# First loads alone, the rest by GpSimd; norm of the input in written order, first two projections by quarters of the tokens

## The chip, the cores and the metric

The kernel runs on one core of one Trainium2 chip. Its time is the device time of one execution in microseconds. Before the change the median of 3 runs is 2382.75 us (2381.59 to 2386.46).

## The reference

A decoder trunk of two layers over 1024 tokens with 1024 channels, float32. In each layer the input is normalized (RMS norm with a gain), projected by one matrix to 3072 columns, and these columns go to four groups of heads: a gated convolution over 31 tokens, a stick-breaking attention, a retention in chunks of 128 tokens and a short gated convolution. The groups' outputs are joined, projected back and normalized, and added to x. A feed-forward part with a convolution over 3 tokens follows.

```python
h = rms_norm(x, norm_mix_pre[l])
proj = h @ w_in[l]                       # 1024 x 1024 by 1024 x 3072
(c_a, c_gate, sb_q, sb_k, sb_v, r_q, r_k, r_v, r_g,
 sc_b, sc_c, sc_h) = jnp.split(proj, N_IN_SLICES, axis=-1)
...
x = x + rms_norm(mix, norm_mix_post[l])
f = conv_ffn(rms_norm(x, norm_ffn_pre[l]), ffn_up[l], ffn_conv_w[l], ffn_down[l])
x = x + rms_norm(f, norm_ffn_post[l])
```

The change concerns `h` and the first 2 of the 24 column blocks of `proj`, in the first layer only.

## The kernel before, in words

**Operands in two parts.** Each float32 operand of a large product is split into a high part, rounded to the type that TensorE multiplies fast, and the remainder. `split` (L180) casts the high part on ScalarE (L181) and subtracts on VectorE (L182). A product is then three: high by high, high by low, low by high. `hH` and `hL` hold the normalized input, transposed, in 8 tiles of 128 tokens.

**The start (L551 to L576).** For each of the 8 tiles of 128 tokens a load of 512 KB from SyncE's queue (L560), `norm` (L165: on ScalarE a sum of squares at L151, logarithm at L156, exponential at L158; on VectorE the scaling by factor and gain at L167), eight transposes on TensorE (L177, against the identity `ident`) into an accumulator or a `tp` tile, as `X0` says, and the split. The identity and the gain (one row of 4 KB, read 128 times by one load, L186) are issued behind the first tile. At the fifth tile the first two weights are fetched (`prefetch`, L201, which calls `load_weight`, L189: a load of 512 KB into the one buffer `wr`, the cast L193, the subtraction L195 into `wh` and `wl`, two buffers each). Params and constants (L571 to L574) are issued last.

**The order of the work.** The program is a list of instructions. A planner gives each engine its own fixed order by estimated starting times, priorities and the order of the text; within `tc.manual_schedule` the named engines keep the order of the text. Each engine works through its own list and waits at an instruction whose operands or whose place aren't ready. `tc.issue_after(ins)` puts all that a block issues on that instruction's engine behind it.

**The projections.** A projection takes one weight of 1024 x 128 (8 blocks of 128 x 128) and gives 128 columns for all 1024 tokens, in one accumulator of two banks. The first two are made as a pair (`project_pair`, L228, called at L716 in both layers): 24 products of 512 tokens for each of two halves of the tokens and each of two weights, 96 in all. The others follow singly (`project`, L216), their accumulators in turn 0 and 1 (`project(n % 2, ...)`, L726); from the third on TensorE keeps the order of the text (L719). `prefetch` fetches one weight ahead. The first projection gives keys (`stick_k`, L333: for each half of the rows a split from the accumulator, L340, and two loads that copy the parts to the other 64 partitions, L341 and L342), the second gives queries (`stick_q`, L324: L328 on ScalarE, L329 on VectorE), the third values. An accumulator is given to its next user when all instructions that read it are done. The scores of the attention (`stick_scores`, L346: products at L361 and L362, the mask at L364) come in between the products of the third and later projections, at slots that are counted in eighths of a projection.

**Buffers.** `ualloc` and `ufree` (L114, L121) hand out 29 buffers of 512 KB in turn.

Of the kernel before, what the change touches and what calls it, by code (L numbers as in the profile page):

```python
# [7 lines left out]
F32 = mybir.dt.float32  # L8
F32R = mybir.dt.float32r
# [3 lines left out]
P = 128  # L13
D = 1024
T = 1024
KT = D // P
NB = T // P
# [53 lines left out]
WPOOL = []  # L71
UPOOL = ()
SKEW = 0
# [3 lines left out]
XP = 4  # L77
OB = 3
FB = 2
X0 = (0,1,2,None,2,None,2,None)  # L80
# [3 lines left out]


@with_exitstack
def trunk_kernel(ctx, tc, x, w_in, w_out, w_up, w_down, params, gains, consts, rope, out):
    nc = tc.nc
    const = ctx.enter_context(tc.tile_pool(name="const", bufs=1))
    big = ctx.enter_context(tc.tile_pool(name="big", bufs=1))  # L90
    wp = ctx.enter_context(tc.tile_pool(name="wp", bufs=2))
    small = ctx.enter_context(tc.tile_pool(name="small", bufs=8))
    pt = ctx.enter_context(tc.tile_pool(name="pt", bufs=2, space=bass.MemoryType.PSUM))
# [3 lines left out]
    ident = const.tile([P, P], F32, name="ident")  # L97
    par = const.tile([P, DEPTH * NPAR], F32, name="par")
    tri = const.tile([P, P], F32, name="tri")
    ones_c = const.tile([P, P], F32, name="ones_c")  # L100
    ones_b = const.tile([P, P], F32, name="ones_b")
    mask = const.tile([P, P], F32, name="mask")
    gam = const.tile([P, 2], F32, name="gam")
# [10 lines left out]
    def ualloc(dt=F32, shape=(P, T)):  # L114
        s = free.pop(0)
        count[0] += 1
        t = big.tile(list(shape), dt, tag=f"u{s}", name=f"u{s}_{count[0]}")
        slot_of[id(t)] = (s, t)
        return t

    def ufree(*ts):  # L121
        for t in ts:
            free.append(slot_of.pop(id(t))[0])
# [11 lines left out]
    def ptile(slot, shape=(P, T)):  # L135
        pcount[0] += 1
        return pp[0].tile(list(shape), F32, tag=f"pp{slot}", name=f"pp{slot}_{pcount[0]}")
# [7 lines left out]
    hH = const.tile([P, NB, KT, P], F32R, name="hH")  # L145
    hL = const.tile([P, NB, KT, P], F32R, name="hL")
    xs = [dr.tile([T, D], F32, name=f"xs{i}") for i in range(2 * DEPTH - 1)]

    def square_sum(src, junk):
        ss = stile("ss")  # L150
        nc.scalar.activation(junk, src, AF.Square, accum_out=ss)  # L151
        return ss

    def rstd_of(ss):
        ln = stile("ln")
        nc.scalar.activation(ln, ss, AF.Ln, scale=1.0 / D, bias=eps_t)  # L156
        r = stile("r")
        nc.scalar.activation(r, ln, AF.Exp, scale=-0.5)  # L158
        return r
# [5 lines left out]
    def norm(xt, gbc, hh):  # L165
        r = rstd_of(square_sum(xt, hh))
        nc.vector.scalar_tensor_tensor(hh, xt, r, gbc, ALU.mult, ALU.mult)  # L167

    def transpose_h(t, hh, slot):
        n = 4 if slot is None else KT  # L170
        for k in range(0, KT, n):
            if slot is None:
                tp = pt.tile([P, 4, P], F32, tag="t", name="tp")
            else:
                tp = ptile(slot, (P, KT, P))
            for j in range(n):
                nc.tensor.transpose(tp[:, j, :], hh[:, (k + j) * P:(k + j + 1) * P], ident)  # L177
            split(hH[:, t, k:k + n, :], hL[:, t, k:k + n, :], tp)

    def split(h, l, src):  # L180
        nc.scalar.copy(h, src)  # L181
        nc.vector.tensor_sub(l, src, h.bitcast(F32))  # L182

    def gain(i):
        g = ualloc()
        nc.sync.dma_start(g, gains[i].partition_broadcast(P))  # L186
        return g

    def load_weight(src, eng):  # L189
        raw = wp.tile([P, KT, P], F32, tag="wr", name="wr", bufs=WR)  # L190
        nc.sync.dma_start(raw, src)
        wh = wp.tile([P, KT, P], F32R, tag="wh", name="wh")
        nc.scalar.copy(wh, raw)  # L193
        wl = wp.tile([P, KT, P], F32R, tag="wl", name="wl")
        eng.tensor_sub(wl, raw, wh.bitcast(F32))  # L195
        return wh, wl

    queue = []
    ready = []

    def prefetch(n=1):  # L201
        while queue and len(ready) < n:
            with tc.high_priority(offset=HPW):
                ready.append(load_weight(*queue.pop(0)))

    def project_kt(ps, w, kt, halves):
        wh, wl = w
        for w, m in ((wh, hH), (wh, hL), (wl, hH)):
            for half in halves:
                nc.tensor.matmul(  # L210
                    ps[:, half * 512:(half + 1) * 512], w[:, kt, :],
                    m[:, 4 * half:4 * half + 4, kt, :],
                    start=(kt == 0 and m is hH and w is wh),
                    stop=(kt == KT - 1 and w is wl))
# [13 lines left out]
    def project_pair(slots):  # L228

        prefetch(2)  # L230
        ws = [ready.pop(0), ready.pop(0)]
        ps = [ptile(i) for i in slots]
        for half in range(2):
            for p, w in zip(ps, ws):
                for kt in range(KT):
                    project_kt(p, w, kt, (half,))
                if half:
                    prefetch()
        return ps
# [182 lines left out]
    def rope_load(i):  # L422
        c = ualloc()
        nc.sync.dma_start(c, rope[i, 0])
        s = ualloc()
        nc.sync.dma_start(s, rope[i, 1])
        return c, s
# [122 lines left out]

    psum("pp")  # L551
    nc.scalar.preload_act_table_set("natural_log_exp_and_others")
    queue += [(w_in[0, n], nc.gpsimd if n in WPOOL else nc.vector) for n in range(24)]
    hhs = []
    for t in range(NB + SKEW):
        if t == XP:
            prefetch(2)
        if t < NB:
            xt = ualloc()
            nc.sync.dma_start(xt, x[t * P:(t + 1) * P, :])  # L560
            if t == 0:
                nc.sync.dma_start(ident, consts[0])
                g_pre = gain(0)
            hhs.append(ualloc())
            norm(xt, g_pre, hhs[t])
            ufree(xt)
        if t >= SKEW:
            transpose_h(t - SKEW, hhs[t - SKEW], X0[t - SKEW])
            ufree(hhs[t - SKEW])
    ufree(g_pre)  # L570
    nc.sync.dma_start(par, params)  # L571
    for dst, i in ((mask, 1), (tri, 2), (ones_c, 3), (ones_b, 4)):
        nc.sync.dma_start(dst, consts[i])
    nc.sync.dma_start(gam, consts[5, :, 0:2])  # L574
    nc.vector.tensor_copy(identr, ident)
    nc.vector.tensor_copy(maskr, mask)  # L576

# [1 line left out]
    for l in range(DEPTH):  # L579
# [133 lines left out]
        at(LN_SLOT + LN_VAR, lambda: layer_var(L, y, sq))  # L713
        cs = None
        region = ExitStack()
        pair = project_pair((0, 1))  # L716
        for n, (kind, i, col) in enumerate(IN_ORDER):
            if n == REGION:
                region.enter_context(tc.manual_schedule(engines={mybir.EngineType.PE}))  # L719
            if kind in ("rq", "rk"):  # L720
                cs = rope_load((0 if kind == "rq" else 2) + i)
# [42 lines left out]
        g_post, g_pre = gain(4 * l + 1), gain(4 * l + 2)  # L764
# [278 lines left out]
        with tc.manual_schedule(engines={mybir.EngineType.PE}):  # L1043
            nextw = weight_pairs(NPLAIN)
            next(nextw)
            w = list(nextw)
            psum("xyz")
            for j in range(NPLAIN, NF):
# [7 lines left out]
                w = ffn_products(j, w, sums, nextw, freed if end else lambda n: None)  # L1056
# [7 lines left out]
        for ci, ch in enumerate(chunks):  # L1064
            final = ci == len(chunks) - 1
            if final:
# [3 lines left out]
                g_post, g_pre = gain(4 * l + 3), None if last else gain(4 * l + 4)  # L1070
# [91 lines left out]
```

## Time and profile before

| | |
|---|---|
| median of 3 runs | 2382.75 us |
| the profiled execution | 2386.67 us, span 2384.9 us |
| TensorE (PE) busy | 2297.3 us, 96% |
| its weight loads (PEld) | 1885.0 us, 79% |
| VectorE (DVE) | 1674.2 us, 70% |
| ScalarE (ACT) | 1080.7 us, 45% |
| GpSimd (POOL) | 196.5 us, 8% |
| DMA | 209.87 MB, mean 88 GB/s |
| mean granted clock of TensorE | 0.986 |

Engines are named as in the profile: PE, PEld (TensorE's weight loads), DVE, ACT, POOL, SP (SyncE). A row of the timeline has its start in us, its length in us, the engine, the line of the kernel, the operation, what it writes and reads, how many instructions are merged in it, and in brackets the idle time of the engine before it and what ended that. [...]

### The profile page before, as it was taken

What the parts mean: (1) busy time and instruction counts of PE and PEld (TensorE: products, weight loads), DVE (VectorE), ACT (ScalarE), POOL (GpSimd) and SP (SyncE); (2) the same over time, 40 slices, a digit from 0 to 9 for tenths busy, and PEclk for the clock granted to TensorE, in tenths of its full rate; (3) what the DMA queues carried; (4) which work ended last, traced back from release to release, by engine and by line L of the source; (5) the groups of instructions that cost most, each with busy time, mean ns of one, the idle gap of its engine ahead of it and who ended that gap; (6) DMA issues with size and microseconds to landing.
All of it is one profiled execution on the core that took longest, in us unless ns stands there. A gap on an engine that the chain in (4) does not pass through costs nothing.

```text
span 2384.9 us, 26334 instructions
## 1 busy us (share of the span) xinstructions
PE 2297.3 (96%) x10596; PEld 1885.0 (79%) x10596; DVE 1674.2 (70%) x1749; ACT 1080.7 (45%) x1463; POOL 196.5 (8%) x84
## 2 busy tenths in 40 slices
PE   7998999999999999999999989999999999999998
PEld 6876787787888888788778767877888888888886
DVE  4699877559777777644556998775598777774445
ACT  5663565434455445421246535654344554453112
POOL 0000000000000000643210000000000000016420
PEclk9998999999999999999999989999999999999999
DMA  4212212412122224522222122123122222235223
GB/s 150 71 53 63 62 36 88 138 48 92 68 88 89 80 80 143 183 80 98 80 80 71 53 62 62 36 95 135 53 89 80 80 80 89 87 121 176 84 71 124
DMA packets 58810, 209.87 MB, mean 88 GB/s; under 512 B 7104, under 2 KB 7872, under 8 KB 58688
## 3 DMA queue, kind: packets, MB, share of 16 engines
q1 hardware_dynamic: 58688, 208.19, 26.7%
q8 instruction: 83, 1.36, 0.2%
q14 instruction: 39, 0.32, 0.0%
HBM read 159.93 MB, written 39.85 MB: 84 GB/s over the span
## 4 chain that ended last, share of the span: by engine, by line
PE 38%; DVE 7%; ACT 3%; DMA 1%; issue 1%; DVEq 0%; SPq 0%
PE pp L984 10%; PE pp L210 9%; PE ppx L901 8%; PE ppy L901 4%; DVE u L261 2%; PE ppz L901 2%; PE pp L738 1%; DVE u L182 1%; ACT u L151 1%; DMA wr<-in_w_out 1%; PE op L409 1%; DVE u L379 1%; DVE u L167 1%; PE tp L396 0%; DMA wr<-in_w_up 0%
## 5 line engine op out<-in xcount | busy, mean ns | idle before, releaser
L261 DVE SCALAR_TENSOR_TENSOR u<-u,par,u 128x1023 f32<-128x1023 f32 (+10 forms) x280 | 356.3, 1284 | 28.6 <-ACT u L793 24.4
L210 PE MATMUL pp<-hH,wh 128*128 128x512 f32 x960 | 327.2, 411 | 1.0 <-DVE u L182 0.5
L997 DVE TENSOR_TENSOR u<-u,pp 128x1024 f32<-128x1024 f32 x143 | 174.6, 1221 | 209.9 <-PE pp L984 209.8
L210 PE MATMUL pp<-hL,wh 128*128 128x512 f32 x960 | 312.7, 396 | 0.0
L210 PE MATMUL pp<-hH,wl 128*128 128x512 f32 x960 | 311.5, 395 | 0.0
L984 PE MATMUL pp<-u,u 128*128 128x512 f32 x1152 | 266.0, 392 | 6.1 <-ACT u L955 4.6
L984 PEld LDWEIGHTS pp<-u,u 128*128 128x128 f32 x1152 | 216.6, 189 | 52.4 <-ACT u L955 5.4
L974 POOL TENSOR_TENSOR hH<-u,hH 128x1024 fp32r<-128x1024 f32 x24 | 58.1, 2451 | 1946.5 <-ACT hH L973 1946.5
L210 PEld LDWEIGHTS pp<-hL,wh 128*128 128x128 f32 x960 | 183.6, 191 | 40.4
L210 PEld LDWEIGHTS pp<-hH,wl 128*128 128x128 f32 x960 | 183.2, 191 | 40.3
L210 PEld LDWEIGHTS pp<-hH,wh 128*128 128x128 f32 x960 | 172.6, 193 | 37.5 <-issue 5.9
L738 PE MATMUL pp<-u,hH 128*128 128x512 f32 x512 | 140.2, 392 | 0.4 <-ACT u L181 0.4
L984 PE MATMUL pp<-hH 128*128 128x512 f32 x576 | 131.5, 389 | 0.0
L984 PEld LDWEIGHTS pp<-hH 128*128 128x128 f32 x576 | 108.1, 188 | 22.4
L901 PE MATMUL ppx<-u,wh 128*128 128x512 f32 x384 | 118.4, 389 | 0.3 <-ACT u L926 0.3
L793 ACT ACTIVATE u<-u,par 128x1024 f32<-128x1024 f32 x76 | 87.8, 1156 | 67.4 <-DVE u L947 65.6
L738 PEld LDWEIGHTS pp<-u,hH 128*128 128x128 f32 x512 | 95.0, 188 | 20.4 <-ACT u L181 1.2
L195 DVE TENSOR_TENSOR wl<-wr,wh 128x1024 fp32r<-128x1024 f32 x60 | 73.3, 1221 | 50.9 <-ACT wh L193 50.7
L973 ACT CAST u<-u 128x1024 fp32r<-128x1024 f32 x48 | 50.2, 1052 | 128.9 <-DMA u<-in_w_down 85.7
L901 PE MATMUL ppx<-u,hH 128*128 128x512 f32 x352 | 108.4, 389 | 0.0
L193 ACT CAST wh<-wr 128x1024 fp32r<-128x1024 f32 x60 | 63.0, 1051 | 71.3 <-PE pp L210 57.1
L379 DVE TENSOR_TENSOR_SCAN u<-pp,u 128x1023 f32<-128x1023 f32 (+3 forms) x64 | 87.8, 1403 | 0.7
(240 smaller groups left out, 4400.3 us busy)
## 6 DMA issues: line engine op xcount, KB each, us to landing
wr<-in_w_up SPq DMA_DIRECT2D x50, 512.0 KB, 3.5
wr<-in_w_in SPq DMA_DIRECT2D x48, 512.0 KB, 3.5
gd<-u SPq DMA_DIRECT2D x44, 512.0 KB, 2.9
u<-in_w_down SPq DMA_DIRECT2D x44, 512.0 KB, 4.3
u<-gd SPq DMA_DIRECT2D x44, 512.0 KB, 3.9
u<-in_w_up SPq DMA_DIRECT2D x38, 512.0 KB, 4.3
xs<-u SPq DMA_DIRECT2D x24, 512.0 KB, 2.6
u<-xs SPq DMA_DIRECT2D x24, 512.0 KB, 3.4
```

The costliest lines, as they stand in the source:

```text
L193: nc.scalar.copy(wh, raw)
L195: eng.tensor_sub(wl, raw, wh.bitcast(F32))
L210: nc.tensor.matmul(ps[:, half * 512:(half + 1) * 512], w[:, kt, :], m[:, 4 * half:4 * half + 4, kt, :], start=(kt == 0 and m is hH and w i ...
L261: eng.scalar_tensor_tensor(acc[:, lo:hi], src[:, lo - s:hi - s], wc, acc[:, lo:hi], ALU.mult, ALU.add)
L379: nc.vector.tensor_tensor_scan(rev, z[:, o + 1:e + 1][:, ::-1], rev, r[:, e:e + 1], ALU.add, ALU.add)
L738: nc.tensor.matmul(ps[:, hs], a[:, t, k, :], w[:, hs], start=(k == 0 and a is hH and w is wo[k][0]), stop=(k == KT - 1 and a is hL))
L793: nc.scalar.activation(acc, ps, AF.Copy, scale=par[:, w + 2:w + 3])
L901: nc.tensor.matmul(ps, a[:, kt, :], x(m, kt), start=start and kt == 0 and a is wh and m == 0, stop=kt == 3 and a is wl, skip_group_check=True)
L973: nc.scalar.copy(h, raw)
L974: (nc.gpsimd if len(loads) >= 4 else nc.vector).tensor_sub(lo, raw, h.bitcast(F32))
L984: nc.tensor.matmul(ps[:, hs], a[:, ts_], w[:, hs], start=(i == 0 and w is h and a is gh), stop=(i == len(gs) - 1 and a is gl))
L997: nc.vector.tensor_add(facc[t], facc[t], ps)
```

## The change

The gain of the first norm comes as an array of its own, `gain0`, with 128 equal rows. SyncE issues four loads: the first tile of x, the gain, the second tile, the identity. GpSimd copies one element of the first tile (`held`), which waits for that tile, and behind it issues the other tiles of x and the first two weights in the order written, then the third weight, params and the constants. The tiles of x and the two weights each have a buffer of the 29. The three engines TensorE, ScalarE and VectorE run the start in the written order of `step`: N is a norm, X the transposes of a tile, S its split, W a weight's split, M(i, q) the 24 products of projection i over quarter q of the tokens (256 of them), each with a moving operand of 256 columns instead of 512. In the first layer this pair takes the place of `project_pair`.

```diff
--- before.py
+++ after.py
@@ -84,7 +84,7 @@
 
 
 @with_exitstack
-def trunk_kernel(ctx, tc, x, w_in, w_out, w_up, w_down, params, gains, consts, rope, out):
+def trunk_kernel(ctx, tc, x, w_in, w_out, w_up, w_down, params, gains, gain0, consts, rope, out):
     nc = tc.nc
     const = ctx.enter_context(tc.tile_pool(name="const", bufs=1))
     big = ctx.enter_context(tc.tile_pool(name="big", bufs=1))
@@ -186,9 +186,9 @@
         nc.sync.dma_start(g, gains[i].partition_broadcast(P))
         return g
 
-    def load_weight(src, eng):
+    def load_weight(src, eng, dma=None):
         raw = wp.tile([P, KT, P], F32, tag="wr", name="wr", bufs=WR)
-        nc.sync.dma_start(raw, src)
+        (dma or nc.sync).dma_start(raw, src)
         wh = wp.tile([P, KT, P], F32R, tag="wh", name="wh")
         nc.scalar.copy(wh, raw)
         wl = wp.tile([P, KT, P], F32R, tag="wl", name="wl")
@@ -550,28 +550,87 @@
 
     psum("pp")
     nc.scalar.preload_act_table_set("natural_log_exp_and_others")
-    queue += [(w_in[0, n], nc.gpsimd if n in WPOOL else nc.vector) for n in range(24)]
-    hhs = []
-    for t in range(NB + SKEW):
-        if t == XP:
-            prefetch(2)
-        if t < NB:
-            xt = ualloc()
-            nc.sync.dma_start(xt, x[t * P:(t + 1) * P, :])
-            if t == 0:
-                nc.sync.dma_start(ident, consts[0])
-                g_pre = gain(0)
-            hhs.append(ualloc())
-            norm(xt, g_pre, hhs[t])
-            ufree(xt)
-        if t >= SKEW:
-            transpose_h(t - SKEW, hhs[t - SKEW], X0[t - SKEW])
-            ufree(hhs[t - SKEW])
+    xts, raws, hhs, tps, ws0 = {}, [], {}, {}, []
+
+    def load_x(t, eng):
+        xts[t] = ualloc()
+        eng.dma_start(xts[t], x[t * P:(t + 1) * P, :])
+
+    def load_w(eng):
+        raws.append(ualloc(F32, (P, KT, P)))
+        eng.dma_start(raws[-1], w_in[0, len(raws) - 1])
+
+    load_x(0, nc.sync)
+    g_pre = ualloc()
+    nc.sync.dma_start(g_pre, gain0)
+    load_x(1, nc.sync)
+    nc.sync.dma_start(ident, consts[0])
+
+    held = nc.gpsimd.tensor_copy(const.tile([1, 1], F32, name="held"), xts[0][0:1, 0:1])
+    with tc.issue_after(held.ins):
+        load_x(2, nc.gpsimd)
+        load_w(nc.gpsimd)
+        load_x(3, nc.gpsimd)
+        load_w(nc.gpsimd)
+        for t in range(4, NB):
+            load_x(t, nc.gpsimd)
+
+    def begin_norm(t):
+        hhs[t] = ualloc()
+        norm(xts[t], g_pre, hhs[t])
+        ufree(xts[t])
+
+    def begin_transpose(t):
+
+        if X0[t] is None:
+            tps[t] = [pt.tile([P, 4, P], F32, tag="t", name="tp") for _ in range(2)]
+        else:
+            tps[t] = [ptile(X0[t], (P, KT, P))]
+        for k in range(KT):
+            n = KT // len(tps[t])
+            nc.tensor.transpose(tps[t][k // n][:, k % n, :], hhs[t][:, k * P:(k + 1) * P], ident)
+
+    def begin_split(t):
+        n = KT // len(tps[t])
+        for i, tp in enumerate(tps[t]):
+            split(hH[:, t, i * n:(i + 1) * n, :], hL[:, t, i * n:(i + 1) * n, :], tp)
+        ufree(hhs[t])
+
+    def begin_weight(i):
+        wh = wp.tile([P, KT, P], F32R, tag="wh", name="wh")
+        wl = wp.tile([P, KT, P], F32R, tag="wl", name="wl")
+        split(wh, wl, raws[i])
+        ufree(raws[i])
+        ws0.append((wh, wl))
+
+    pair0 = []
+
+    def begin_product(i, quarter):
+
+        if quarter == 0:
+            pair0.append(ptile(i))
+        wh, wl = ws0[i]
+        cs = slice(256 * quarter, 256 * quarter + 256)
+        for n, (w, m) in enumerate(((wh, hH), (wl, hH), (wh, hL))):
+            for kt in range(KT):
+                nc.tensor.matmul(pair0[i][:, cs], w[:, kt, :], m[:, 2 * quarter:2 * quarter + 2, kt, :],
+                                 start=(n == 0 and kt == 0), stop=(n == 2 and kt == KT - 1))
+
+    with tc.manual_schedule(engines={mybir.EngineType.PE, mybir.EngineType.Activation, mybir.EngineType.DVE}):
+        N, X, S, W, M = begin_norm, begin_transpose, begin_split, begin_weight, begin_product
+        for step in ((N, 0), (X, 0), (N, 1), (S, 0), (X, 1), (N, 2), (W, 0), (S, 1), (X, 2), (M, 0, 0),
+                     (N, 3), (W, 1), (S, 2), (X, 3), (M, 1, 0), (N, 4), (S, 3), (X, 4), (M, 0, 1),
+                     (N, 5), (S, 4), (X, 5), (M, 1, 1), (N, 6), (S, 5), (X, 6), (M, 0, 2), (N, 7), (S, 6),
+                     (X, 7), (M, 1, 2), (S, 7), (M, 0, 3), (M, 1, 3)):
+            step[0](*step[1:])
     ufree(g_pre)
-    nc.sync.dma_start(par, params)
-    for dst, i in ((mask, 1), (tri, 2), (ones_c, 3), (ones_b, 4)):
-        nc.sync.dma_start(dst, consts[i])
-    nc.sync.dma_start(gam, consts[5, :, 0:2])
+    queue += [(w_in[0, n], nc.vector, nc.gpsimd if n == 2 else nc.sync) for n in range(2, 24)]
+    with tc.issue_after(held.ins):
+        prefetch()
+        nc.gpsimd.dma_start(par, params)
+        for dst, i in ((mask, 1), (tri, 2), (ones_c, 3), (ones_b, 4)):
+            nc.gpsimd.dma_start(dst, consts[i])
+        nc.gpsimd.dma_start(gam, consts[5, :, 0:2])
     nc.vector.tensor_copy(identr, ident)
     nc.vector.tensor_copy(maskr, mask)
 
@@ -713,7 +772,7 @@
         at(LN_SLOT + LN_VAR, lambda: layer_var(L, y, sq))
         cs = None
         region = ExitStack()
-        pair = project_pair((0, 1))
+        pair = project_pair((0, 1)) if l else pair0
         for n, (kind, i, col) in enumerate(IN_ORDER):
             if n == REGION:
                 region.enter_context(tc.manual_schedule(engines={mybir.EngineType.PE}))
@@ -1150,6 +1209,7 @@
     arrays, args = {}, []
     for name, v in (("x", a["x"].reshape(T, D)), ("w_in", w_in), ("w_out", a["w_out"]), ("w_up", w_up),
                     ("w_down", a["ffn_down"]), ("params", np.concatenate(par, axis=1)), ("gains", gains),
+                    ("gain0", np.broadcast_to(gains[0], (P, D))),
                     ("consts", consts), ("rope", rope)):
         v = np.ascontiguousarray(v)
         arrays["in_" + name] = v
```

## Rows read from the trace of the kernel before

**Rows 1.** Stretches: the start, and one of the first layer.

```profile
0.00:22.35 22.35, 7.27 (x32) 6.24 (x32) 10.38 (x11) 15.10 (x32) 0.20 (x4) 1.00 0.72 256
...
110.00:260.00 150.00, 130.16 (x640) 106.05 (x639) 143.52 (x160) 73.46 (x94) 0.00 (x0) 0.93 0.22 64
```

**Rows 2.** Timeline of the start, all engines.

```profile
4.49 1.06 ACT L151 ACTIVATE u<-u 128x1024 f32<-128x1024 f32 x1 [2.47 <-DMA u<-in_x]
...
6.00 0.20 ACT L158 ACTIVATE r<-ln 128x1 f32<-128x1 f32 x1
8.72 1.28 DVE L167 SCALAR_TENSOR_TENSOR u<-u,r,u 128x1024 f32<-128x1024 f32 x1 [3.79 <-DMA u<-in_gains]
...
10.06 1.97 PE L177 MATMUL pp<-ident,u 128*128 128x128 f32 x8 [10.06 <-DVE u L167]
...
12.57 0.99 ACT L181 CAST hH<-pp 128x1024 fp32r<-128x1024 f32 x1
...
13.59 1.23 DVE L182 TENSOR_TENSOR hL<-pp,hH 128x1024 fp32r<-128x1024 f32 x1 [0.65 <-ACT hH L181]
...
22.35 0.50 PE L210 MATMUL pp<-hH,wh 128*128 128x512 f32 x1 [0.50 <-ACT hH L181]
...
25.63 0.90 PEld L177 LDWEIGHTS tp<-ident,u 128*128 128x128 f32 x8 [0.17 <-issue]
...
26.50 0.19 PEld L210 LDWEIGHTS pp<-hH,wl 128*128 128x128 f32 x1
```

**Rows 3.** Stretches of half a microsecond: the DMA engines.

```profile
5.50:6.00 0.50, 0.00 (x0) 0.00 (x0) 0.00 (x0) 0.43 (x4) 0.00 (x0) 1.00 0.91 238
...
8.50:9.00 0.50, 0.00 (x0) 0.00 (x0) 0.28 (x1) 0.00 (x0) 0.00 (x0) 1.00 1.02 418
```

**Rows 4.** Timeline of SyncE's queue.

```profile
3.55 0.44 SPq L191 DMA_DIRECT2D wr<-in_w_in  x1
...
9.90 0.33 SPq L571 DMA_DIRECT2D par<-in_params  x1
```

**Rows 5.** Groups by line: GpSimd's costliest (busy us, mean ns).

```profile
L974 POOL TENSOR_TENSOR u<-u,u 128x1024 fp32r<-128x1024 f32 x32 | 76.5, 2405 | 58.1 <-PE pp L984 27.4 <-ACT u L973 22.4 <-issue 8.1
```

**Rows 6.** Timeline of TensorE: products of 512 and of 256 columns.

```profile
73.03 0.62 PE L210 MATMUL pp<-hH,wl 128*128 128x512 f32 x2
73.48 1.12 PE L409 MATMUL op<-u,u 128*128 128x256 f32 x8
74.43 0.63 PE L210 MATMUL pp<-hH,wh 128*128 128x512 f32 x2
```

**Rows 7.** Timeline: eviction of the first projection, start of the third.

```profile
42.90 1.06 ACT L193 CAST wh<-wr 128x1024 fp32r<-128x1024 f32 x1 [9.12 <-PE pp L210]
...
43.86 1.00 ACT L181 CAST u<-pp 64x1024 fp32r<-64x1024 f32 x1
...
45.13 1.21 DVE L182 TENSOR_TENSOR u<-pp,u 64x1024 fp32r<-64x1024 f32 x1
...
46.38 1.01 ACT L181 CAST u<-pp 64x1024 fp32r<-64x1024 f32 x1 [1.51 <-DVE u L182]
...
47.42 1.23 DVE L182 TENSOR_TENSOR u<-pp,u 64x1024 fp32r<-64x1024 f32 x1 [1.08 <-ACT u L181]
...
48.79 0.70 PE L210 MATMUL pp<-hH,wh 128*128 128x512 f32 x2 [0.27 <-DVE u L182]
```

**Rows 8.** Stretches: two waits of TensorE and what follows each.

```profile
953.73:956.74 3.01, 0.00 (x1) 0.01 (x1) 2.97 (x4) 3.01 (x5) 0.00 (x0) 0.98 0.42 161
956.74:960.30 3.56, 3.56 (x9) 2.84 (x10) 3.56 (x2) 2.79 (x3) 2.59 (x2) 0.54 0.00 0
...
583.28:588.96 5.68, 0.00 (x1) 0.03 (x1) 5.65 (x6) 2.58 (x3) 0.00 (x0) 0.91 0.14 57
588.96:595.00 6.04, 6.04 (x15) 4.74 (x16) 2.41 (x3) 0.54 (x1) 0.00 (x0) 0.52 0.21 87
```

**Rows 9.** Timeline of TensorE: the first scores.

```profile
55.71 0.39 PE L361 MATMUL pp<-u,u 128*128 128x512 f32 x1
```

## The prediction

> **What bounds the kernel now.** I read the page's first part (TensorE is far ahead of the rest), then stretches of the start, then the timeline of that stretch, then TensorE's waits. In the first 22.35 us TensorE is idle for 15.1; from 110 to 260 VectorE is full (143.5 of 150 us) and TensorE waits for it [rows 1]. The change touches only the first 49 us. The timeline shows what ends last there [rows 2]: the first tile of x is there at 4.49, its norm's factor at 6.20, but the scaling waits for the gain until 8.72; the transposes begin at 10.06, and the first product, over tokens 0 to 511, at 22.35. The third projection starts at 48.79. All later work follows TensorE's order from that point: VectorE's long convolutions feed on projections still to come, so a shift at 48.79 moves the full stretch too. What I forecast is the shift of that one start.
>
> **Loads.** The gain is now read from an array with 128 rows instead of one row 128 times. While it was under way the DMA engines were busy 0.91 at 238 GB/s; behind it 1.02 at 418 [rows 3]. At 418 GB/s a 512 KB tile takes 1.3 us, so behind x0 (4.5) I put the gain at 5.8, x1 at 7.1, the identity at 7.2. The other loads wait for x0 on GpSimd and queue there: a one-element copy, then x2, w0, x3, w1, x4 to x7, the third weight, params and constants. SyncE is rid of 15 issues of 0.33 to 0.44 us [rows 4]. GpSimd issues no DMA in this trace. The bounds for one issue there are SyncE's 0.33 us and the 2.4 us of GpSimd's nearest instruction [rows 5]; up to 1.3 the wire hides it. I take 1.3: x2 8.5, w0 9.8, x3 11.1, w1 12.4, then one per 1.3. Worked through at 2.4, the end of the stage moves by 0.1 us only, since TensorE uses one tile in some 3.8 us.
>
> [...]
>
> **The written order.** A norm is 1.71 us on ScalarE (4.49 to 6.20), the scaling 1.28, eight transposes 1.97 at the slow clock and, once warm, 0.87 to their successor; a split is 1.0 on ScalarE and 1.23 on VectorE [rows 2], a weight the same. In order: norm 0 ready 6.2, scaled 7.5, transposed 7.55 to 9.5. Norm 1 from 7.1, scaled 10.1, transposed 10.15 to 12.1. ScalarE: split 0 at 9.6, norm 2 at 10.5 (scaled 13.5), weight 0 at 12.1, split 1 at 13.05. Transposes 2 from 13.55 to 15.5, and there the first quarter begins: 15.5 against 22.35. Its last third needs the low half of split 1, done by 16, so it doesn't stop.
>
> A product of 256 columns costs 0.119 us to its successor (eight from 73.48 to 74.43), one of 512 0.226 (two from 73.03) [rows 6]. Thus 192 halves instead of 96 wholes is 22.9 against 21.7 us, 1.2 more. A quarter is 24 x 0.119 = 2.87 us.
>
> [...]
>
> The first quarter, partly at the slow clock, I give 0.3 more: it ends at 18.7. Behind it stand, back to back, five tiles' transposes (5 x 0.92 = 4.6) and six quarters (17.2): the fourth quarter of projection 0 ends at 40.5, that of projection 1 at 43.3. Norms and splits (2.7 us of ScalarE and 2.5 of VectorE a tile) stay ahead of TensorE's 3.8. Bounds: the clock full already at 12 gives 39.3 for projection 0, not before 19 gives 41.9.
>
> **The new wait.** Projections 0 and 2 share an accumulator (slot n % 2), so the third can't start before all of the first is evicted. Before, the first ended at 42.90, and one piece followed another: third weight cast 42.90, key high 43.86, low 45.13, high 46.38, low 47.42 to 48.65, TensorE on at 48.79 [rows 7]: 5.9 us. The second projection's last half lay over it (24 x 0.226 = 5.4 us), so only 0.4 us were lost. Now only a quarter, 2.87 us, lies over it. TensorE stands from 43.3 until 40.5 + 5.9 = 46.4. If ScalarE takes the first query's piece (1.0 us like the key's, ready at 43.4) ahead of the second key's, both engines lose some 0.75 more: 47.1. If the key went ahead of the weight, it would be 1 earlier: 45.4. I take 46.8, a gain of 2.0 us, not the 5 by which the products end earlier. Behind the waiting product stands everything of TensorE; nothing else is ready for it, since scores need the queries.
>
> **The clock.** TensorE would stand for 3.5 us. [...]
>
> **Moved without cost.** The constants and params come by GpSimd after x7, some 17 to 25 us; the mask's first use is with the scores at 55.71, 6.9 behind the third projection's start [rows 9]. The key's low half is sent to its other partitions at about 44 and needed at 53.7. The third weight's cast needs the buffer of weight 0, free at 40.5, and lies in the eviction chain counted above. One input more changes nothing inside the span.
>
> **Sum.** -2.0 + 1.8 = -0.2 us. The profiled execution, 2386.67 for a span of 2384.9, stands 3.9 above the median 2382.75 of runs between 2381.59 and 2386.46; the difference applies to any of them: 2382.5. What a measurement can tell from no change is 0.2%, 4.8 us.
>
> **Rivals.**
> (1) The stage is quicker and the wait shorter. With the clock up by 14 us projection 0 ends at 39.6; with the key cast first the third starts at 44.5, 4.3 earlier, after 2.1 us of standing, over which the clock may hold: 2378.4. For it: both are choices of a planner and of the clock that the rows don't fix. Against it: before, the weight went first [rows 7].
> (2) Slower: GpSimd's issues become the bound. Above about 2.5 us for each of its first eight loads they set the stage, since weight 1 and the tiles then come later than TensorE asks; from there on the change is slower than before. At 3.5 us (x2 10.7, w0 14.2, x3 17.7, w1 21.2) projection 0 ends at 46.0 and the third starts at 52.1, 3.3 late; with the clock's 1.8, 2387.9. [...]
> (3) It does as said, but the planner, whose starting times have changed, orders VectorE's and ScalarE's work otherwise between 110 and 260, where VectorE is full: one piece of 1.2 us more or less ahead of each of some four waits of TensorE is 5 us either way, 2378 or 2388. Against it: behind the third projection the same work stands in the same order, only shifted.
>
> **How the numbers follow.** Forecast 0.60, (1) 0.17, (2) 0.13, (3) 0.10. The forecast's own bounds: third start 45.2 to 48.2, loss by the clock 0 to 2.9, so 2379 to 2385; 0.04 of its 0.60 lies over 4.8 us faster, 0.03 slower. Faster by over 0.2%: 0.04 + half of (1), 0.09, + 0.06 of (3) = 0.19. Slower: 0.03 + 0.08 of (2) + 0.04 of (3) = 0.15. Within: 0.66. The range takes in the forecast, (1) but for its end, and (2) up to 3.5 us an issue: 2376.5 to 2388.
>
> **What would show it.** The first scaling at about 6.2, the first product near 15.5, the last of the pair near 43. Then one wait of TensorE on VectorE's split, 3 us long, where there was 0.3, with the third projection's first products 0.44 apart. If the third starts by 45 at the full clock, (1) holds; if norms wait for x3 to x7, (2). Wrong altogether would be a third projection that starts as the pair's products end, 43.5, or a difference that arises behind 110 us.

## The result, and the profile after

| | median us | lowest to highest | runs |
|---|---|---|---|
| before | 2384.61 | 2381.59 to 2386.62 | 4 |
| after | 2407.6 | 2401.16 to 2411.72 | 4 |

The ratio is 1.0095, with a 95% interval from 1.0069 to 1.0121: 23 us slower, where no change was forecast. The profiled execution is the fastest of the four (2401.16 us, span 2399.4) and stands against one of before that was among its slowest (2386.67), so the two traces show 14.5 us of the 23.

The start went nearly as forecast. The timeline of the changed kernel (the columns of [rows 2]), its start and then the eviction of the first projection [rows 7]:

```profile
4.56 0.17 POOL L569 COPY held<-u 1x1 f32<-1x1 f32 x1 [4.11 <-DMA u<-in_x]
4.68 0.71 POOL L557 DMA_DIRECT2D u<-in_x  x1
5.38 0.54 POOL L561 DMA_DIRECT2D u<-in_w_in  x1
...
6.27 1.28 DVE L167 SCALAR_TENSOR_TENSOR u<-u,r,u 128x1024 f32<-128x1024 f32 x1 [5.40 <-ACT r L158]
...
15.23 2.06 PE L616 MATMUL pp<-hH,wh 128*128 128x256 f32 x8
...
41.07 1.05 ACT L193 CAST wh<-wr 128x1024 fp32r<-128x1024 f32 x1 [5.03 <-PE pp L616]
...
42.76 1.10 PE L616 MATMUL pp<-hL,wh 128*128 128x256 f32 x8
...
43.90 1.02 ACT L328 ACTIVATE u<-pp 64x1024 fp32r<-64x1024 f32 x1 [0.88 <-PE pp L616]
...
44.95 1.01 ACT L181 CAST u<-pp 64x1024 fp32r<-64x1024 f32 x1
44.95 1.22 DVE L329 SCALAR_TENSOR_TENSOR u<-pp,u 64x1024 fp32r<-64x1024 f32 x1 [0.45 <-ACT u L328]
...
46.20 1.23 DVE L182 TENSOR_TENSOR u<-pp,u 64x1024 fp32r<-64x1024 f32 x1
...
47.48 0.73 PE L210 MATMUL pp<-hH,wh 128*128 128x512 f32 x2 [3.62 <-DVE u L182]
...
49.04 1.05 PE L210 MATMUL pp<-hH,wh 128*128 128x512 f32 x2
49.89 1.05 PE L210 MATMUL pp<-hL,wh 128*128 128x512 f32 x2
...
56.12 0.39 PE L361 MATMUL pp<-u,u 128*128 128x512 f32 x1
```

The scaling comes at 6.27 (8.72 before), the first product at 15.23 (22.35), the pair's last group at 42.76. TensorE then waits 3.62 us for the second half of the keys, since ScalarE took the query's piece (43.90) ahead of it, and VectorE too (44.95). Two products take 0.85 us from 49.04 on (49.04, 49.89, 50.74), about half the speed of [rows 6], where two take 0.45 (73.03 to 73.48). The first scores stand at 56.12, 0.41 later than before [rows 9].

Stretches after, with the columns of [rows 1] (the stretch, its length, the busy time of PE, PEld, DVE, ACT and POOL with the number of instructions, the granted clock of TensorE as a share of full speed, the mean busy share of the DMA engines, and the GB/s that they moved):

```profile
0.00:22.35 22.35, 12.67 (x73) 11.88 (x74) 13.49 (x14) 16.12 (x31) 8.46 (x20) 1.00 0.83 306
110.00:260.00 150.00, 134.53 (x643) 108.47 (x643) 144.38 (x160) 73.45 (x95) 0.00 (x0) 0.92 0.23 66
...
47.48:56.12 8.64, 8.64 (x30) 6.87 (x31) 2.43 (x2) 1.05 (x1) 0.00 (x0) 0.80 0.49 129
```

The third projection took 8.64 us at a granted clock of 0.80; before, from 48.79 to 55.71, 6.92 at 1.00. In 110 to 260 TensorE was busy for 134.53 us instead of 130.16 [rows 1]: the same products take longer there. The view of one line's instructions names them (number, then shortest, median and longest duration in ns, first and last start; the last number counts a sample). Before:

```profile
L738 PE MATMUL pp<-u,hH x512: 387/389/501, 409.6 to 1705.0; 128*128 128x512 f32 x171
...
L901 PE MATMUL ppx<-u,hH x352: 389/389/389, 602.7 to 2123.4; 128*128 128x512 f32 x176
L901 PE MATMUL ppx<-u,u x264: 389/389/389, 635.3 to 2129.0; 128*128 128x512 f32 x132
...
L901 PE MATMUL ppy<-hH,wh x64: 389/389/389, 624.4 to 2112.3; 128*128 128x512 f32 x64
...
L901 PE MATMUL ppx<-hH x64: 389/389/389, 629.9 to 2117.7; 128*128 128x512 f32 x64
...
L984 PE MATMUL pp<-u,u x1152: 387/389/794, 956.7 to 2377.6; 128*128 128x512 f32 x192
```

After (L797, L960 and L1043 are the same lines):

```profile
L797 PE MATMUL pp<-u,hH x512: 388/396/478, 410.6 to 1710.3; 128*128 128x512 f32 x171
...
L960 PE MATMUL ppx<-u,hH x352: 392/395/399, 604.2 to 2136.5; 128*128 128x512 f32 x176
...
L960 PE MATMUL ppx<-u,u x264: 387/389/398, 637.4 to 2142.2; 128*128 128x512 f32 x132
L960 PE MATMUL ppy<-hH,wh x64: 395/396/397, 626.3 to 2125.2; 128*128 128x512 f32 x64
...
L960 PE MATMUL ppx<-hH x64: 389/393/397, 631.9 to 2130.7; 128*128 128x512 f32 x64
...
L1043 PE MATMUL pp<-u,u x1152: 387/389/504, 964.4 to 2391.1; 128*128 128x512 f32 x192
```

A product's tiles stand in the order moving operand, stationary operand. Products that pair `hH` or `hL` with a `u` buffer or a weight take 394 to 396 ns where 389 was, over both layers; `u` by `u` is still at 389. (`hH` by `hH` takes 393, though both its operands are in `hH`; the fourth experiment says why.) The edit touches none of these lines, but it makes a new tile: `held = const.tile([1, 1], ...)`. It takes 32 bytes of each partition right behind `hL` in the compiled program. So the 29 `u` buffers, `wr`, `wh` and `wl` all lie 32 bytes further on (the last three also change places, by whole multiples of 4096 bytes), and `hH` and `hL` do not.

### The profile page after: what moved, and what is told of

It is laid out like the page before. It is cut to its first block, busy times and chain, and to the rows that moved or that the text cites. A ratio compares the mean times of both kernels' runs of the same rounds, so it can differ in the third digit from the quotient of the medians.

```text
span 2399.4 us, 26539 instructions
## 1 busy us (share of the span) xinstructions
PE 2323.0 (97%) x10692; PEld 1888.3 (79%) x10692; DVE 1676.0 (70%) x1749; ACT 1081.1 (45%) x1463; POOL 204.9 (9%) x100
## 5 line engine op out<-in xcount | busy, mean ns | idle before, releaser
L210 PE MATMUL pp<-hH,wh 128*128 128x512 f32 x928 | 318.2, 416 | 3.7 <-DVE u L182 3.6
L210 PE MATMUL pp<-hL,wh 128*128 128x512 f32 x928 | 304.0, 400 | 0.0
L210 PE MATMUL pp<-hH,wl 128*128 128x512 f32 x928 | 303.1, 399 | 0.0
L1043 PE MATMUL pp<-u,u 128*128 128x512 f32 x1152 | 264.6, 390 | 5.7 <-ACT u L1014 4.2
L1043 PEld LDWEIGHTS pp<-u,u 128*128 128x128 f32 x1152 | 215.5, 188 | 51.8 <-ACT u L1014 5.0
L210 PEld LDWEIGHTS pp<-hL,wh 128*128 128x128 f32 x928 | 177.6, 191 | 42.9
L210 PEld LDWEIGHTS pp<-hH,wl 128*128 128x128 f32 x928 | 177.0, 191 | 42.7
L210 PEld LDWEIGHTS pp<-hH,wh 128*128 128x128 f32 x928 | 166.1, 192 | 41.1 <-issue 5.6
L797 PE MATMUL pp<-u,hH 128*128 128x512 f32 x512 | 142.8, 397 | 0.0
L1043 PE MATMUL pp<-hH 128*128 128x512 f32 x576 | 131.6, 389 | 0.0
L1043 PEld LDWEIGHTS pp<-hH 128*128 128x128 f32 x576 | 108.1, 188 | 22.6
L960 PE MATMUL ppx<-u,wh 128*128 128x512 f32 x384 | 118.9, 391 | 0.0
L797 PEld LDWEIGHTS pp<-u,hH 128*128 128x128 f32 x512 | 95.1, 188 | 22.2
L960 PE MATMUL ppx<-u,hH 128*128 128x512 f32 x352 | 110.5, 395 | 0.0
```

The lines of the kernel that those rows point to most:

```text
L210: nc.tensor.matmul(ps[:, half * 512:(half + 1) * 512], w[:, kt, :], m[:, 4 * half:4 * half + 4, kt, :], start=(kt == 0 and m is hH and w i ...
L797: nc.tensor.matmul(ps[:, hs], a[:, t, k, :], w[:, hs], start=(k == 0 and a is hH and w is wo[k][0]), stop=(k == KT - 1 and a is hL))
L960: nc.tensor.matmul(ps, a[:, kt, :], x(m, kt), start=start and kt == 0 and a is wh and m == 0, stop=kt == 3 and a is wl, skip_group_check=True)
L1043: nc.tensor.matmul(ps[:, hs], a[:, ts_], w[:, hs], start=(i == 0 and w is h and a is gh), stop=(i == len(gs) - 1 and a is gl))
```

## The experiments

Theory A: that shift of one operand against the other makes the products slower, whatever the start does. Rival B: the new start does it (order of the engines, buffers in another turn, GpSimd). Below, "interval" is the mean time from one 512-column product's start to the next one's, over all in the trace between 0.20 and 0.26 us, worked out from the records.

**The tile 64 bytes wide.** The changed kernel with

```diff
-    held = nc.gpsimd.tensor_copy(const.tile([1, 1], F32, name="held"), xts[0][0:1, 0:1])
+    held_t = const.tile([1, 16], F32, name="held")
+    held = nc.gpsimd.tensor_copy(held_t[:, 0:1], xts[0][0:1, 0:1])
```

> The changed kernel, its one-element tile made 64 bytes wide instead of 4 (which take 32), so that all buffers behind it lie 64 bytes further than before the change and not 32. Theory A (products whose two operands differ by 32 bytes modulo 64 are slower: 0.232 to 0.234 us to the next where it was 0.227, all through the run): products of 512 columns back at 0.227, the start as in the changed kernel (third projection at 47.5, scores about 56.0), and the whole within 3 us of before, about 0.3 above it. Rival B (the written order, GpSimd's loads or another order of instructions slow TensorE): still 14 to 25 us above before.

2403.89 us, 1.0083 [1.0065, 1.01]. A shift of 64 bytes costs as much as one of 32. So the period of 64 bytes that the expectation had put into theory A is out, and by this run alone rival B would do as well.

**32 bytes behind `hL` in the kernel before**, all else as it was:

```diff
     hL = const.tile([P, NB, KT, P], F32R, name="hL")
+    pad = const.tile([1, 8], F32, name="pad")
+    nc.vector.memset(pad, 0.0)
```

> The kernel before, with nothing but a tile of 32 bytes (set to zero once) between hL and the 29 buffers; start, loads and order stay. Theory A: 13 to 23 us slower than before, products with one operand in hH or hL and the other behind the tile at 0.231 to 0.235 us, down projections (both operands on one side) at 0.227. Rival B: within 1 us of before.

2402.66 us, 1.0082 [1.0064, 1.0099]. The old start, and nearly the whole loss: B is out as its main cause.

**The same 32 bytes ahead of `hH`**, so that all large buffers move together:

```diff
+    pad = const.tile([1, 8], F32, name="pad")
+    nc.vector.memset(pad, 0.0)
     hH = const.tile([P, NB, KT, P], F32R, name="hH")
```

> The kernel before, with the tile of 32 bytes ahead of hH: hH, hL, the 29 buffers and the weights all lie 32 bytes further, none of them differs from another by 32 modulo 64. Theory A (the difference of the two operands counts): within 2 us of before, 0.227 everywhere. Rival C (an operand that starts at 32 modulo 64 is slower in itself): at least 15 us slower, down projections too, since every operand is shifted.

2384.87 us, 1.0005 [0.9991, 1.0019]: no change. The place itself doesn't count, only the distance between large operands, and rival C is out.

**32 bytes between the `u` buffers and the weights:**

```diff
     big = ctx.enter_context(tc.tile_pool(name="big", bufs=1))
+    padp = ctx.enter_context(tc.tile_pool(name="padp", bufs=1))
...
+    pad = padp.tile([1, 8], F32, name="pad")
+    nc.vector.memset(pad, 0.0)
```

> The kernel before, with the tile of 32 bytes between the 29 buffers and the weights wr, wh, wl. Theory A: slow are only products of wh or wl with hH, hL or a buffer: the projections (0.232 to 0.235) and the feed-forward products with wh and wl (0.230 to 0.235); the output projection (hH by a buffer) and the down projection stay at 0.227. In all some 10 to 16 us slower. Rival C: slow are the products that read wh or wl, to the same 10 to 16 us, so this run tells the two apart only together with the one where everything is shifted.

2398.52 us, 1.0059 [1.0039, 1.008]. The products that slow down change places, in the same view of one line's instructions:

```profile
L904 PE MATMUL ppx<-u,wh x384: 392/395/502, 598.2 to 2144.4; 128*128 128x512 f32 x192
L904 PE MATMUL ppx<-u,hH x352: 389/389/397, 603.8 to 2133.4; 128*128 128x512 f32 x176
...
L741 PE MATMUL pp<-u,hH x512: 387/389/504, 410.3 to 1709.5; 128*128 128x512 f32 x171
```

`u` by `wh` is slow now and `u` by `hH` is back at 389: with the shift put elsewhere, the other pairs pay. That shows the distance between operands as the cause.

The records also tell which two operands. In the feed-forward and down products TensorE's load of the next product's stationary operand starts some 3 ns after each product's start and takes 188. In the run with 32 bytes behind `hL`, 54 of these had their own two operands on one side of the shift, and the next product had both of its operands on the other side: all 54 took 235 ns to the next start, where the kernel before has 226 or 227. Another 68 had their own two on one side and were followed by a product with its operands on both sides, the stationary one on theirs: all 68 took 226 or 227. So what pays is a moving operand against the stationary operand that is loaded while it is read, that of the next product; in a run of like products this is the distance between a product's own two. Behind such a run some eight more products still take 228 to 233 ns on average, and so `hH` by `hH` shows 393.

**128, 256 and 512 bytes behind `hL`** (the second experiment with `[1, 32]`, `[1, 64]`, `[1, 128]`):

> The kernel before with 128 bytes more between hL and all later buffers, nothing else. If the period is 128 bytes or shorter: 2381 to 2388, products at 0.227 us throughout; 32 and 64 bytes each cost some 20 us, so a period of 64 bytes is out already. If it is longer than 128, or there is none: 2396 to 2406 and 0.230 to 0.234 us.

> The kernel before with 256 bytes more between hL and all later buffers, nothing else. 32, 64 and 128 bytes made it some 20 us slower, 512 bytes did not. If the place counts modulo 256 bytes: 2380 to 2388 and products at 0.227 us throughout. If modulo 512: 2396 to 2406 and 0.232 to 0.234 us for products with operands from both sides.

> The kernel before with 512 bytes more between hL and all later buffers, nothing else. Theory A as 'any shift between the two operands costs': 2396 to 2406, products with operands from both sides at 0.232 to 0.234 us. Rival (only a shift that isn't a multiple of some short period costs, and 512 bytes are a multiple of it): 2381 to 2388, products at 0.227 us throughout.

128 bytes: 2400.35 us, 1.0069 [1.0056, 1.0082]. 256: 2383.48, 1.0002 [0.9992, 1.0012]. 512: 2385.71, 1.0008 [0.9996, 1.0019]. Of the five sizes tried the two that are multiples of 256 cost nothing that can be measured, so the place counts modulo 256 bytes as far as these sizes tell. So theory A as 'any shift costs', put beside the run with 512, is out. One line each with 128 and with 256 bytes:

```profile
L903 PE MATMUL ppx<-u,hH x352: 387/394/398, 605.6 to 2137.1; 128*128 128x512 f32 x176
```

```profile
L903 PE MATMUL ppx<-u,hH x352: 389/389/389, 600.3 to 2117.7; 128*128 128x512 f32 x176
```

The intervals in ns, with the shift in bytes of `u` and of the weights against `hH` and `hL` (the last two columns are products into `ppx`):

| kernel | `u`, weights | projection hH,wh | output projection u,hH | feed-forward u,hH | feed-forward u,wh |
|---|---|---|---|---|---|
| before | 0, 0 | 228.6 | 227.3 | 226.7 | 226.8 |
| after | 32, 32 | 233.0 | 233.2 | 233.1 | 228.5 |
| 64 bytes wide | 64, 64 | 233.5 | 229.0 | 231.7 | 228.4 |
| 32 behind | 32, 32 | 233.0 | 233.2 | 233.1 | 228.3 |
| 32 ahead | 0, 0 | 228.5 | 227.2 | 226.6 | 226.7 |
| ahead of the weights | 0, 32 | 233.0 | 227.4 | 227.0 | 232.9 |
| 128 behind | 128, 128 | 232.5 | 232.8 | 232.9 | 227.5 |
| 256 behind | 256, 256 | 228.7 | 227.4 | 226.7 | 226.7 |
| 512 behind | 512, 512 | 228.6 | 227.4 | 226.8 | 226.9 |

**The change without its shift:** `held` in the pool of small tiles, behind all large buffers.

```diff
-    held = nc.gpsimd.tensor_copy(const.tile([1, 1], F32, name="held"), xts[0][0:1, 0:1])
+    held = nc.gpsimd.tensor_copy(stile("held")[0:1], xts[0][0:1, 0:1])
```

> The changed kernel, but its one-element tile `held` lies in the pool of small tiles behind all large buffers, so that nothing else is shifted against hH and hL. Theory A (the shift alone is what the change lost; the start itself nets nothing): the third projection starts near 47.5 us with its first products at half the clock, the first scores at 55.8 to 56.1, products of 512 columns are back at 0.227 us to their successor in every part, and the time is within 3 us of the kernel before: 2381 to 2386. Rival B (the new start changes something that lasts: the order of the engines, GpSimd's loads, buffers handed out in another turn): the products are back at 0.227 us but 10 us or more of the loss stay: 2394 or above. Rival C (the products are slow for another reason than the place of the tile): 0.232 to 0.234 us and 2400 or above.

2387.51 us (2381.21 to 2393.43, 12 runs) against 2383.29, 1.0012 [1.0001, 1.0023]. The intervals are those of before (228.7, 227.4, 226.7, 226.7). So theory A holds: the shift has most of the loss. The time is 1.5 us above what A expected, and some 4 above the kernel before, where the interval of the ratio only just leaves 1 out. In its timeline the wait stands (3.62 us), and the slow products behind it (two in 0.82 to 0.86 us from 48.40 to 51.78):

```profile
43.09 1.12 PE L616 MATMUL pp<-hL,wh 128*128 128x256 f32 x8
47.83 0.74 PE L210 MATMUL pp<-hH,wh 128*128 128x512 f32 x2 [3.62 <-DVE u L182]
48.40 1.03 PE L210 MATMUL pp<-hL,wh 128*128 128x512 f32 x2
...
56.38 0.39 PE L361 MATMUL pp<-u,u 128*128 128x512 f32 x1
```

**The wait taken away:** the same, with the split of tile 7 and the last quarter of projection 0 ahead of the third quarter of projection 1.

```diff
-                     (X, 7), (M, 1, 2), (S, 7), (M, 0, 3), (M, 1, 3)):
+                     (X, 7), (S, 7), (M, 0, 3), (M, 1, 2), (M, 1, 3)):
```

> As the run before it (held behind all buffers), and besides the order of the end of the start is changed: the split of tile 7 and the fourth quarter of projection 0 come ahead of the third quarter of projection 1, so that two quarters of projection 1, 5.7 us, lie over the eviction of projection 0's accumulator (5.9 to 6.7 us) instead of one. If the forecast's reading of the wait is right: TensorE stands about 1.2 us for the split of tile 7 ahead of that quarter and under 1 us ahead of the third projection instead of 3.6, the third projection starts 1 to 2 us earlier (45.5 to 46.5) and keeps the full clock, which is 1.8 us more; the first scores at 52.5 to 53.5 and 2 to 4 us less than the run before it: 2378 to 2382. Rival D (the clock falls after the short wait as well, or the wait just moves ahead of the quarter): the first scores at 55 or later and no difference from the run before it.

2380.64 us (2378.54 to 2387.2, 12 runs), 0.9991 [0.9981, 1.0001]. In the timeline there is no wait ahead of the third projection, and its granted clock is 1.00 (44.25 to 51.18):

```profile
43.06 1.12 PE L616 MATMUL pp<-hL,wh 128*128 128x256 f32 x8
44.25 0.73 PE L210 MATMUL pp<-hH,wh 128*128 128x512 f32 x2
...
51.18 0.39 PE L361 MATMUL pp<-u,u 128*128 128x512 f32 x1
```

The scores come 5.2 us ahead of the run before it: 3.58 at the third projection's start (47.83 to 44.25), and 1.62 in its length (8.55 to 6.93). By medians it is 6.9 us. The expected 52.5 to 53.5 was too late: the two quarters cover all of the eviction, which took 5.7 us (38.46 to 44.19) with no piece of the query in between, and the wait for the split of tile 7 was 0.24 us instead of 1.2.

**Loads by SyncE again**, none held back (the kernel with `held` behind, each `nc.gpsimd` of the start's loads replaced by `nc.sync`):

> The changed kernel with `held` behind all buffers, and all loads of the start issued by SyncE in the same order, none held back for the first tile (SyncE takes 0.33 to 0.44 us an issue, GpSimd 0.53 to 0.71). If holding the loads back is what brings the first scaling to 6.3: x0 and the gain share the DMA engines with what follows, the first scaling comes at 7 to 9, the first quarter at 16 to 18, and the third projection 0.5 to 2.5 us later than 47.5 to 47.8. If only the gain's new form counts: the first scaling at 6.2 to 6.6 and all milestones within 0.4 us. The time in both cases 2382 to 2390.

2386.17 us, 1.0012 [0.9997, 1.0026]; the first scaling at 6.33, the first quarter at 15.30, the third projection at 47.47, the scores at 56.02. So the second case held. SyncE issues seven other loads before x0 is used at 4.59; with the loads held back it was three, and x0 was used at 4.53 in the changed kernel and 4.57 with `held` behind. Holding them back and moving them to GpSimd brings nothing and costs nothing that shows.

**The gain array alone**, in the kernel before:

```diff
             if t == 0:
+                g_pre = ualloc()
+                nc.sync.dma_start(g_pre, gain0)
                 nc.sync.dma_start(ident, consts[0])
-                g_pre = gain(0)
```

> The kernel before with one part of the change alone: the gain of the first norm as an array of 128 rows, loaded behind the first tile and ahead of the identity. Loads by SyncE, the planner's order and the pair in halves of 512 tokens stay, so 24 products of 512 columns, 5.4 us, still lie over the eviction of the first accumulator. If the late gain alone set the start: the first scaling at 6.2 to 6.4 instead of 8.72, all of the start 2 to 2.5 us earlier, no new wait ahead of the third projection, the first scores at 52.5 to 54 (54.5 to 55.8 in the runs with the order of before), the time 2378 to 2383. If the tiles that follow or the planner's new order set it: the first scaling earlier all the same, the first product later than 21.5, the scores at 54.5 to 56 and 2381 to 2387.

2379.51 us (2377.3 to 2389.1, 11 runs) against 2382.15, 0.9991 [0.9982, 1.0]. In its timeline:

```profile
6.08 1.28 DVE L167 SCALAR_TENSOR_TENSOR u<-u,r,u 128x1024 f32<-128x1024 f32 x1 [5.22 <-ACT r L158]
...
45.68 0.70 PE L210 MATMUL pp<-hH,wh 128*128 128x512 f32 x2 [0.26 <-DVE u L182]
...
52.58 0.39 PE L361 MATMUL pp<-u,u 128*128 128x512 f32 x1
```

The third projection starts 3.1 us earlier than in the trace of before, with a wait of 0.26: half a pair, 5.4 us, still covers the eviction. By the first scores one part of the change brings 3.1 us, and the most that any order of the whole start brought below is 5.0; in the medians the two can't be told apart.

**The first quarter earlier still** (tile 7 first; the first quarter ahead of norm 2 and transposes 2, the transposes in pairs):

```diff
-        for step in ((N, 0), (X, 0), (N, 1), (S, 0), (X, 1), (N, 2), (W, 0), (S, 1), (X, 2), (M, 0, 0),
...
+        for step in ((N, 0), (X, 0), (N, 1), (S, 0), (X, 1), (W, 0), (S, 1), (M, 0, 0), (N, 2), (N, 3), (W, 1),
+                     (X, 2), (S, 2), (X, 3), (M, 1, 0), (S, 3), (N, 4), (M, 0, 1), (N, 5), (N, 6), (X, 4), (S, 4),
+                     (X, 5), (M, 1, 1), (S, 5), (N, 7), (X, 6), (S, 6), (X, 7), (M, 0, 2), (S, 7),
+                     (M, 0, 3), (M, 1, 2), (M, 1, 3)):
```

> The order with the split of tile 7 first, `held` behind all buffers, and the start reordered once more: the first quarter ahead of the transposes of tile 2 and ahead of norm 2 on ScalarE, the transposes in pairs. Worked out from the rows of the run with tile 7 first: the first weight's high part at 11.7, split 1 at 12.2 to 13.2, so the first quarter at 13.2 instead of 15.25; no wait ahead of the third projection; the first scores at 49.5 to 51.5 (51.2 with tile 7 first), the time 2376 to 2382. If the transposes then wait for norms, the gain is lost: scores at 51 to 53.

2380.88 us (12 runs) against 2383.62, 0.9996 [0.9987, 1.0005]. The quarter starts at 13.07 instead of 15.25, its second group still at the slow speed (from 14.95 on, 1.80 us long, the third 1.11); the scores at 50.74, 0.44 earlier than with tile 7 first. The rest of the 2.2 goes mostly to the slow second group and to a wait of 0.5 for a norm.

Three kernels have medians 2.6 or 2.7 us under before (tile 7 first, this one, the gain array alone), and the upper ends of their intervals lie between 1.0 and 1.0005. All are clearly faster than the changed kernel; that one of them beats the kernel before is not shown.

## Why the prediction was wrong

**The step that failed** is "What I forecast is the shift of that one start", with "All later work follows TensorE's order from that point": a product at 0.226 us [rows 6] was taken as fixed for all of that work. `held` was costed as an instruction, "a one-element copy", and not as a tile that has a place; "Moved without cost" looks at loads and at the new input, not at what the new tile moves. The prediction's test for "wrong altogether", a difference that arises behind 110 us, is what came.

What the runs showed in its place: with `held` behind `hL` a product of 512 columns took 0.233 us to its successor in the projections and output projections and 0.231 in the feed-forward part, and with `held` elsewhere 0.227 to 0.228 again. The size, from the intervals of the old kernel with and without 32 bytes: 2662 products of projections by 4.6 ns are 12.3 us, 740 of output projections by 5.9 are 4.3, 3182 of the feed-forward part by 4.3 are 13.7 (about 1 to 7, by pair), 2096 of the down projection by 0.1 are 0.3. Together 30.6 us, for the 19.5 measured (2402.66 less 2383.17). In 110 to 260, where TensorE waits for VectorE, the slower products mostly shortened its waits: it is busy 4.4 us longer (134.53 against 130.16), yet the first output projection starts just 0.6 us later against the first scores than before.

**Loads: right; the holding back wasn't needed for it.** 6.27 came as forecast (6.2). GpSimd's issues took 0.53 to 0.71 us each, inside the bounds of 0.33 and 2.4; rival (2) is out. SyncE's took 0.33 to 0.54 us in the run with the loads by SyncE. The scores came 0.36 us earlier there, less than two traces of one start differ by (below). What brought the early scaling is the gain's array, not the holding back.

**The written order: right.** 15.23 against 15.5; the last group at 42.76 and 43.7 its end, against 43.3.

**The new wait: right in kind, 0.7 to 1.0 late.** 47.48 or 47.83 for 46.8. ScalarE took the query's piece first, the later of the prediction's cases (47.1), and VectorE then did the same (44.95 ahead of 46.20). The wait is 3.62 us for 3.5.

**The clock: right.** After a wait of 3.01 us the granted clock was 0.54 for 3.56 us, after one of 5.68 it was 0.52 for 6.04 [rows 8]; by that, an estimate, 1.6 and 2.9 us of work are lost. The sum's 1.8, for a wait of 3.5 us, was the author's choice near the first; no run shows that figure. In its place the runs showed, behind waits of 3.62 us, a granted clock of 0.80 over the third projection: 8.64 against 6.92 us is 1.7, of which 0.15 is the slower products' own (30 by some 5 ns); 8.55 against 6.93 without the shift is 1.62.

**The sum of the start: too good by 0.5 to 2.1 us.** Without the shift the first scores stand at 56.38 and, with the loads by SyncE, at 56.02. The prediction's gain of 2.0 was taken against one trace of the old start, with the third projection at 48.79 and the scores at 55.71. The old start in the three other traces that have the operands at their old distance (32 bytes ahead, 256 and 512 behind) has 48.25, 47.65 and 47.56, and the scores at 55.17, 54.57 and 54.47. So the new start loses 0.3 to 1.9 us there, where a gain of 0.2 was forecast. The median says +4 [+0.2, +5.5 by the interval]; that there is more in it than the start's own loss isn't shown.

The traces differ by more than the medians, 14.9 us between `held` behind and tile 7 first, but the first is the slowest of its twelve runs (2393.43) and the second the fastest of its twelve (2378.54). Of it 5.2 stand at the first scores, and one more can be placed. The stretch between the same two products with `held` behind, and then with tile 7 first:

```profile
136.00:150.00 14.00, 13.10 (x61) 10.71 (x61) 12.97 (x15) 7.44 (x10) 0.00 (x0) 0.88 0.30 76
```

```profile
131.00:144.00 13.00, 11.70 (x61) 9.76 (x62) 12.85 (x14) 7.48 (x10) 0.00 (x0) 1.00 0.31 82
```

The same 61 products, 1 us longer, at 0.88 instead of 1.00. The clock fell there with the loads by SyncE too (0.88 from 136 to 150), but this isn't of the new start: it was 0.88 from 134 to 148 with 32 bytes behind `hL` and 0.89 from 130 to 146 with the gain array alone, both with the old order, and it didn't fall there in the changed kernel (1.00 from 136 to 150). Some 2 us more arise between 210 and 413, about TensorE's waits for VectorE, and 6.6 behind that. Why the clock falls in one run and not in another stays open. Rival (3), another order of the engines, is out: from the first score on TensorE, VectorE, ScalarE and GpSimd run the same instructions, by line and tile (buffer numbers left out), in the same order in the kernel before, the changed one and the one with `held` behind.

## What to carry to other kernels

A new tile can cost by its place, not only by its instruction: 32 and 128 bytes behind `hL` cost 0.8% and 0.7% here (1.0082 and 1.0069), 256 and 512 nothing that shows (1.0002 and 1.0008). Put small tiles behind the large buffers, or pad them so that the large operands keep their distance modulo 256 bytes, as far as the sizes tried here tell, and compare the durations of products that the edit doesn't touch. Where an accumulator is shared, the work that lies over its eviction counts, not the end of the products: finer pieces uncovered it here (a wait of 3.62 us for 0.27), and a change of two steps in the written order covered it again. Before a start is rebuilt, try its one late operand alone.

## What the runs showed of the hardware that was not expected

- A 512-column product whose moving operand lies 32 or 128 bytes off its old distance from the next product's stationary operand took medians of 394 to 396 ns instead of 389, and some 233 ns instead of 227 from start to start; 256 and 512 bytes off took nothing. Why the distance of these two counts, and why modulo 256, the runs don't show.
- With 64 bytes the output projection pays less (229.0) than with 32 or 128 (233.2 and 232.8), while the projections pay in full (233.5), and of the 54 products named in the fourth experiment 53 took 225 or 226 ns; not explained.
- Products of 256 columns don't follow it: eight took 0.95 us in the changed kernel (41.81 to 42.76) and 0.96 with the shift taken out (42.13 to 43.09).
- x0 was used about as early with seven other loads issued behind it (4.59) as with three (4.53 and 4.57).
- The granted clock of the rows reads 1.00 in the first 22.35 us [rows 1], though eight transposes take 1.97 us there and 0.87 later [rows 2]. The slow speed of the start is read from the durations; that column doesn't show it.
